# A gated two-branch decoder layer on one core: each weight block loaded once from ScalarE's queue, and gates that meet the branch outputs on chip

## The chip, the cores and the metric

The kernel runs on one core of one Trainium2 chip. The metric is the device time in microseconds (us) of one execution, here simply the time of that core. Engines are called as in the profile: PE (TensorE matmul) with PEld (its weight load), DVE (VectorE), ACT (ScalarE), POOL (GpSimd) and SP (SyncE, which here does nothing but issue DMAs). A row of the profile that begins with SPq is SP handing a DMA to its queue.

## The reference, cut to what matters

```python
D_MODEL = 1024; SEQ = 2048; HG_HEADS = RET_HEADS = 8; HG_DK = 128; RET_DK = 64
h    = rms_norm(x, norm_g) * (1 + scale) + shift          # shift, scale, gate from c @ w_ada
proj = h @ w_in                                           # (2048, 1024) @ (1024, 9216)
(hq, hf, hi, hz, rq, rk, rv, rz, ga, gb) = split(proj)
oA = hgrn2_chunkwise(hq, hf, hi, lower_bounds)            # gated linear recurrence, 8 heads
uA = head_rms_norm(oA, hg_norm_g) * silu(hz)
oB = retention_chunkwise(rotary(rq), rotary(rk), rv)      # decayed linear attention, 8 heads
uB = head_rms_norm(oB, ret_norm_g) * silu(rz)
m  = sigmoid(ga) * uA + sigmoid(gb) * uB
out = rms_norm(x + gate * (m @ w_out), final_g)
```

All of it is in float32.

## The kernel before

**Quads and products.** The projection is done over two superblocks of 1024 positions (`sb`), each of two blocks of 512 (`tb`). Its 9216 columns are cut into 36 "quads" of 256 columns, and a quad of one superblock is a 2x2 arrangement of blocks: two column halves (`ch`) by two position blocks (`tb`). It is computed with seven products instead of eight (a Strassen scheme), numbered m = 1 to 7. The weight of a quad has four blocks, 0 to 3 (128 columns by half of the 1024 rows each); the seven products need block 0 (m=1), block 2 (m=2 and, later, part of a sum), block 3 (m=3), a sum of blocks 0 and 1 (m=5), that sum plus block 3 (m=6), that plus block 2 (m=4), and block 1 plus block 3 (m=7). Each operand is split into a high and a low part (`split_into`: a copy on ACT, then a subtraction on DVE), and a product is 4 x 3 matmuls of 128x128 by 128x512: the group "x12" of the timelines. The split weights wait in the tiles `b`, of which there are three (NBW), so that splits run about three products ahead of PE.

**Kinds of quads.** There are five: "a" (query and forget gate of an HGRN2 head), "v" (values of both branches of a head), "b" (queries and keys of a pair of retention heads, to be rotated), "A" and "B" (the gates of a head's HGRN2 and retention output). `quads_of` sets them in the order a, v, (b for even heads), A, B, head after head. `product_order` interleaves the products of neighbouring quads: ... (1,q) (3,q) (6,q) (2,q+1) (7,q) (5,q+1) (4,q) ... `after` turns a finished product into one of the four results of its quad and passes it on to `take_a`, `take_v`, `take_b` or `take_g`. The last result, of m=4, is read straight from the PSUM bank in which PE summed it (`x`), and the bank is free for the next quad's product when that reading is done.

**Weights.** `Weights.load` issues all loads from SP (256 KB each, tiles `w`, `wz`, `wt`, `wt5n`, `wt6n`). The sums of blocks are made by loading a block a second or third time into a temporary and adding it on DVE (`add`, line 401). In all nine loads per quad.

**Background.** Between the products, a scheduler in the program (`bg`, one burst every GAP ticks, four ticks per product) emits the recurrences: `tree` (the decay tree of a head, matmuls `lv`), `hgrn_out` (chunks `poh`, which read `vh` from DRAM), `retention` (chunks `rt` and `por`, which read `rqk`, `rkz` and `vr`). Layout changes go through DRAM: values are stored in 128-byte pieces to `vd`, rotated keys to `kzd`, branch outputs to `ud`. `merges` reads a head's stored gate (`gd` to `mg`) and output (`ud` to `mu`), multiplies and adds them and stores `mT`, which the last stage (`out_half`, matmuls `ops`) reads.

**Rotation.** `tables` writes the cosines and sines of all positions to `rot` by 128 small DRAM-to-DRAM copies (line 618). `take_b` loads `ct` and `sn` from it when a result of a b quad arrives, then multiplies the result with them on DVE (lines 629 to 632); the result of m=4 stays in its PSUM bank meanwhile:

```python
        ct, sn, sw = tmp(f"ct{nm}"), tmp(f"sn{nm}"), tmp(f"sw{nm}")
        nc.sync.dma_start(out=ct, in_=rot[0, b])
        nc.sync.dma_start(out=sn, in_=rot[1, b])
```

Every engine and every queue works through its instructions in the order in which they stand; that order is made when the program is built. All DMAs of the kernel before are issued by SP.

## Time and profile before

| | |
|---|---|
| median of two runs | 2619.3 us (2616.39 to 2622.2) |
| profiled execution | 2623.15 us, of which the span from first to last instruction is 2621.3 us |
| PE busy | 2008.0 us (77% of the span) |
| DVE, ACT, POOL busy | 1537.3, 941.4, 203.4 us |
| mean granted TensorE clock | 0.883 of full speed |
| DMA | 426.20 MB, mean 163 GB/s; 16 DMA engines busy 59% of the span |

The page has the busy time of the engines, then the span in 40 slices, the DMA queues, the chain of work that ended last, and groups of instructions. A group's row gives the line, engine, operation, output and input names and shapes, the count, busy time and mean duration in ns, and after the second bar the idle time of the engine before these instructions with what ended it. A wait row says which engine and line waited for which: total us, times, longest.

### The profile page before, as it was taken

Reading aid. Unit: us, or ns where it says so; the run is one execution under the profiler, and the core shown is the slowest. Engines: PE = TensorE matmul, PEld = TensorE weight load, DVE = VectorE, ACT = ScalarE, POOL = GpSimd, SP = SyncE. Lnnn points to the kernel's source line nnn. Section 1 sums busy time; section 2 is a strip of 40 time slices with the busy share of each in tenths; the row PEclk is TensorE's granted clock in tenths of the full one; section 3 lists DMA queues with packets and bytes.
Section 4 is the critical chain, followed back from the end, with each engine's and each line's share of the span. In section 5 each row is a group of like instructions: output and inputs, shape, how many; then the busy total and the mean of one; then the engine's idle time right before and its main releaser. Section 6 shows DMA issues by size and latency. Waiting matters only on the chain. (4 is left out here: it accounts for less than half of the span.)

```text
span 2621.3 us, 40791 instructions
## 1 busy us (share of the span) xinstructions
PE 2008.0 (77%) x14648; PEld 1596.4 (61%) x14648; DVE 1537.3 (59%) x2935; ACT 941.4 (36%) x2340; POOL 203.4 (8%) x386
## 2 busy tenths in 40 slices
PE   4337998589866887487675998589867888497998
PEld 2226776477745766375564776367655666375877
DVE  5327576557555666566665666557564766467443
ACT  5312343244423453243532443134423343145332
POOL 1000001000100111000010001000100011000200
PEclk9668999799888998798787999789988999798999
DMA  7125566555656576577865556555666566556763
GB/s 251 41 66 149 148 176 147 143 169 155 158 151 172 147 221 171 155 243 223 237 154 136 156 152 159 147 153 156 162 154 169 152 196 168 146 155 176 190 174 127
DMA packets 904986, 426.20 MB, mean 163 GB/s; under 512 B 419920, under 2 KB 829520, under 8 KB 904784
## 3 DMA queue, kind: packets, MB, share of 16 engines
q1 hardware_dynamic: 904784, 423.60, 59.3%
q8 instruction: 116, 1.90, 0.3%
q14 instruction: 86, 0.70, 0.1%
HBM read 321.73 MB, written 103.81 MB: 162 GB/s over the span
## 5 line engine op out<-in xcount | busy, mean ns | idle before, releaser
L82 PE MATMUL x<-S,b 128*128 128x512 f32 x1704 | 453.4, 412 | 173.0 <-ACT b L303 161.4
L82 PEld LDWEIGHTS x<-S,b 128*128 128x128 f32 x1704 | 331.4, 199 | 254.0 <-ACT b L303 169.2
L82 PE MATMUL x<-A,b 128*128 128x512 f32 x1704 | 440.4, 409 | 23.7 <-DVE c L498 6.3
L82 PE MATMUL v<-S,b 128*128 128x512 f32 x1728 | 449.4, 405 | 8.5 <-DVE b L304 6.4
L82 PEld LDWEIGHTS x<-A,b 128*128 128x128 f32 x1704 | 328.9, 197 | 98.0 <-ACT A L303 7.2
L82 PEld LDWEIGHTS v<-S,b 128*128 128x128 f32 x1728 | 330.2, 195 | 80.8 <-DVE b L304 7.7
L82 PE MATMUL y<-A,b 128*128 128x512 f32 x852 | 247.4, 440 | 157.5 <-DVE ct L631 109.7
L82 PEld LDWEIGHTS y<-A,b 128*128 128x128 f32 x852 | 178.5, 215 | 204.4 <-issue 142.9
L304 DVE TENSOR_TENSOR b<-w,b 128x512 fp32r<-128x512 f32 (+1 forms) x320 | 199.8, 634 | 130.8 <-ACT b L303 128.1
L303 ACT ACTIVATE b<-wz 128x512 fp32r<-128x512 f32 (+1 forms) x240 | 137.8, 584 | 295.4 <-DVE wz L401 203.6
L303 ACT ACTIVATE b<-w 128x512 fp32r<-128x512 f32 (+1 forms) x320 | 183.0, 583 | 163.3 <-PE x L82 80.8
L304 DVE TENSOR_TENSOR b<-wz,b 128x512 fp32r<-128x512 f32 (+1 forms) x240 | 150.4, 635 | 120.6 <-ACT b L303 118.8
L82 PE MATMUL ops<-wo,m 128*128 128x512 f32 x768 | 179.7, 394 | 7.7 <-ACT m L303 4.8
L82 PEld LDWEIGHTS ops<-wo,m 128*128 128x128 f32 x768 | 144.7, 190 | 39.5 <-ACT m L303 5.2
L181 POOL TENSOR_SCALAR ssh<-ssh 128x1 f32<-128x1 f32 x128 | 38.4, 300 | 1501.3 <-ACT jkh L802 1501.2
L474 ACT ACTIVATE c<-v 128x512 f32<-128x512 f32 x144 | 85.7, 595 | 157.4 <-PE v L82 157.0
L802 ACT ACTIVATE jkh<-poh 128x128 f32<-128x128 f32 x128 | 35.2, 275 | 265.9 <-DVE st L871 209.2
L401 DVE TENSOR_TENSOR wz<-wz,wt5n 128x512 f32<-128x512 f32 x72 | 49.5, 687 | 120.2 <-DMA wt5n<-in_w_a_dram 81.2
L733 DVE TENSOR_TENSOR q<-q,f 128x512 f32<-128x512 f32 x112 | 77.0, 688 | 48.2 <-PE lv L82 47.0
L184 POOL TENSOR_TENSOR rrr<-ssr,mhalf 128x2 f32<-128x2 f32 x64 | 51.1, 799 | 620.6 <-DVE ssr L183 503.6
L82 PE MATMUL poh<-vh,k 128*128 128x128 f32 x240 | 53.9, 308 | 51.4 <-DMA vh<-vd 40.7
L82 PEld LDWEIGHTS lv<-q,k 128*32 128x32 f32 (+1 forms) x5888 | 73.0, 113 | 30.3 <-issue 24.3
(186 smaller groups left out, 2599.2 us busy)
## 6 DMA issues: line engine op xcount, KB each, us to landing
w<-in_w_d_dram SPq DMA_DIRECT2D x128, 256.0 KB
w<-in_w_a_dram SPq DMA_DIRECT2D x64, 256.0 KB
w<-in_w_c_dram SPq DMA_DIRECT2D x64, 256.0 KB
vd<-vt SPq DMA_DIRECT2D x256, 64.0 KB
wt<-in_w_d_dram SPq DMA_DIRECT2D x64, 256.0 KB
gd<-c SPq DMA_DIRECT2D x64, 256.0 KB
ud<-ut SPq DMA_DIRECT2D x64, 256.0 KB
mg<-gd SPq DMA_DIRECT2D x64, 256.0 KB
```

The lines of the kernel that those rows point to most:

```text
L82: return tc.keep_in_program_order(nc.tensor.matmul(**kw))
L181: G.tensor_scalar(out=ss, in0=ss, scalar1=1.0 / n, scalar2=EPS, op0=ALU.mult, op1=ALU.add)
L184: G.tensor_tensor(out=dst, in0=ss, in1=mhalf.broadcast_to([P, width]), op=ALU.pow)
L303: S.activation(out=t[0], in_=src, func=AF.Copy)
L304: return V.tensor_tensor(out=t[1], in0=src, in1=t[0], op=ALU.subtract)
L401: V.tensor_tensor(out=t, in0=t, in1=w, op=ALU.add)
L474: S.activation(out=t, in_=ps, func=AF.Copy)
L733: V.tensor_tensor(out=qv, in0=qv, in1=tv[:, :, :, 0:1].broadcast_to([P, NU, nb, m]), op=ALU.mult)
L802: S.activation(out=junk, in_=pos[i], func=AF.Square, accum_out=ss[:, i : i + 1])
```

## The change

- **Weights.** Each block is loaded once per quad (of a superblock) into one of five tiles `r`; only blocks 0 and 2 of the first three quads are loaded a second time. The loads are issued from ScalarE's queue (line 404 of the changed kernel). The sums are made from the resident tiles: before the split of m=5 the sum of blocks 0 and 1, before the split of m=6 block 3 is added to it, after that split block 2 gets the sum added (for m=4) and block 1 gets block 3 added (for m=7). That is four DVE additions per quad, as before.
- **Order of quads.** A written-out order (`ORDER`) puts a head's gate quads A and B about two heads later. A gate's product chain now ends on chip: `fetch_u` loads the stored branch output (`mu`) shortly before, and `take_g` multiplies gate, gain and output and adds the two branches; `merges`, `gd` and the reloads `mg` are gone.
- **Rotation.** `tables` writes 12 copies to a compact table `lin`; `load_rot` loads `ct` and `sn` once per block of positions of a b quad, with a broadcast read, before the products m=1 and m=6 of that quad. The rotation of the m=4 result uses tables that were loaded before.
- **Fewer transfers.** `vr` of two heads is one DMA instead of two, and it and `rkz` are fetched one burst before they are used.
- **Constants.** Factors 1/n and the like are folded into other constants; the eps addition of the retention norm moves from DVE to POOL. The junk output of the squares goes to PSUM. GAP goes from 8 to 7, temporaries (NTP) from 7 to 5, with four tiles `mu`.

```diff
-NR = 3
-NZ = 2
+NR = 5
-NTP = 7
+NTP = 5
-GAP = 8.0
+GAP = 7.0
+ORDER = """a0 v0 b0 v1 a1 b1 v2 a2 A0 B0 v3 a3 A1 B1 v4 b2 a4 A2 B2 v5 a5 A3 B3 v6 b3 a6 A4 B4 v7 a7 A5 B5 B6 A6 B7 A7"""
...
-        def add(self, t, q, b, nm):
-                w = tmp(f"wt{nm}")
-                nc.sync.dma_start(out=as_src(w), in_=wsrc(q, b))
-                V.tensor_tensor(out=t, in0=t, in1=w, op=ALU.add)
...
+        def load(self, reserve=1):
+            while self.nload < len(self.order) and self.free > reserve:
+                q, b = self.order[self.nload]
+                t = self.raw[q, b] = self.tile(f"w{q}_{b}")
+                nc.scalar.dma_start(out=as_src(t), in_=wsrc(q, {11: 0, 12: 2}.get(b, b)))
                 self.nload += 1
...
+                if m == 5:
+                    b11, b12 = have(q, 0), have(q, 1)
+                    z = self.raw[q, 5] = self.tile(f"wz{q}")
+                    self.add(z, b11, b12)
+                elif m == 6:
+                    self.add(have(q, 5), have(q, 5), have(q, 3))
...
+                if m == 6:
+                    self.add(have(q, 2), have(q, 2), have(q, 5))
+                    self.add(have(q, 1), have(q, 1), have(q, 3))
...
-                        nc.sync.dma_start(
-                            out=rot[i, b][32 * g : 32 * g + 32, :].rearrange("d (c j a) -> j d c a", j=4, a=32)[j],
...
+                for j in range(4):
+                    nc.sync.dma_start(
+                        out=lin[i + two].rearrange("d (c j a) -> j d c a", j=4, a=32)[j],
...
+    def load_rot(q, tb):
+        nc.sync.dma_start(out=ct, in_=lin[0, :, sl].unsqueeze(0).broadcast_to([4, 32, BLK]))
+        for two in range(2):
+            nc.sync.dma_start(
+                out=sn[64 * two : 64 * two + 64, :], in_=lin[1 + two, :, sl].unsqueeze(0).broadcast_to([2, 32, BLK])
+            )
...
     def take_b(sb, p, s, tb, z):
-        ct, sn, sw = tmp(f"ct{nm}"), tmp(f"sn{nm}"), tmp(f"sw{nm}")
-        nc.sync.dma_start(out=ct, in_=rot[0, b])
-        nc.sync.dma_start(out=sn, in_=rot[1, b])
+        ct, sn = rots[tb]
...
-        nc.sync.dma_start(out=gd[s, h, b], in_=g)
-        gsent[s, h, b] = bg.now
+        u = mus.pop((s, tb))
+        V.scalar_tensor_tensor(
+            out=u, in0=g, scalar=gnt[:, s * H + h : s * H + h + 1], in1=u, op0=ALU.mult, op1=ALU.mult
+        )
...
+        if kind in "AB" and m in (2, 1):
+            fetch_u(q, 2 - m)
+        if kind == "b" and m in (1, 6) and q >= FIRST:
+            load_rot(q, m // 6)
```

**What moves on SP at the start.** Before, in SP's order right after the cosines and sines have come in (`tabd` holds the turned tables, `wt5n` and `wt6n` are weight blocks for sums):

```order
L618 DMA rot_2_313<-tabd_0_817 128x1x32 x16
L618 DMA rot_2_317<-tabd_0_823 128x1x32 x8
L618 DMA rot_2_317<-tabd_1_826 128x1x32 x8
L618 DMA rot_3_314<-tabd_0_817 128x1x32 x16
L618 DMA rot_3_318<-tabd_0_823 128x1x32 x8
L618 DMA rot_3_318<-tabd_1_826 128x1x32 x8
L400 DMA wt5n_975<-in_w_a_dram 128x4x128
L400 DMA wt6n_984<-in_w_a_dram 128x4x128
L400 DMA wt5n_1004<-in_w_c_dram 128x4x128
```

The same place on SP in the changed kernel, from the tables to the first stores of values:

```order
L614 DMA tab_725<-in_cos_dram 128x512
L614 DMA tab_733<-in_sin_dram 128x512
L621 DMA lin<-tabt_726 512x1x32 x4
L621 DMA lin<-tabt_734 512x1x32 x4
L621 DMA lin<-tab_733 512x1x32 x4
L632 DMA ct_0_746<-lin 128x1x512
L634 DMA sn_0_747<-lin 64x1x512 x2
L599 DMA vd_0_122<-vt_0_0_0_858 32x16x32 x4
```

The 128 small copies are 12, and no weight stands behind them.

**What moves on SP at a b quad.** Before, at the third b quad of the first superblock (`rd` and `kzd` are stores of rotated results, `dk` and `k` the tree's turned keys; `w_22`, `wz`, `wt5n` and `wt_22` weights):

```order
L639 DMA rd_0_286<-ct_2_0_6456 2x32x512 x2
L1005 DMA mu_3_1_6527<-ud_3_1_167 32x16x32 x3
L1003 DMA mg_3_1_6533<-gd_3_1_263 128x512
L1005 DMA mu_3_1_6534<-ud_3_1_199 32x16x32 x4
L627 DMA ct_2_0_6562<-rot_0_311 128x512
L628 DMA sn_2_0_6563<-rot_0_315 128x512
L419 DMA wz_6680<-in_w_d_dram 128x4x128
L411 DMA w_22_6730<-in_w_d_dram 128x4x128
L784 DMA dk_0_0_6786<-f_0_5772 128x512
L400 DMA wt5n_6576<-in_w_d_dram 128x4x128
```

The third b quad in the changed kernel, on SP:

```order
L632 DMA ct_0_4976<-lin 128x1x512
L634 DMA sn_0_4977<-lin 64x1x512 x2
L599 DMA vd_0_130<-vt_4_0_1_4974 32x16x32 x4
L874 DMA vh_0_4_5028<-vd_0_128 128x128
L655 DMA rd_0_214<-c_15_4885 2x32x512 x2
L632 DMA ct_1_5050<-lin 128x1x512
L634 DMA sn_1_5051<-lin 64x1x512 x2
L860 DMA ud_3_0_158<-ut_3_0_5041 128x512
```

The tables of the first block of positions now stand ahead of the quad's first store and those of the second right behind it, and no weight stands in this queue. In all, SP has 2,557 DMAs before and 1,582 after.

**What moves on ACT.** ScalarE's order before, with the numbers in the names, at the quad behind that b quad (`b1_22` is the high part of the split weight for m=1 of quad 22, `c2` and `c5` are copies of finished products out of PSUM, `sz` the sigmoid of a gate):

```order
L303 ACTIVATE b5_22_6845<-wz_22_6680 128x512
L659 ACTIVATE sz0_4_0_6795<-c2_21_6640 128x512
L474 ACTIVATE c2_22_6867<-y22_6844 128x512
L303 ACTIVATE b4_21_6869<-wz_21_6324 128x512
L303 ACTIVATE b1_22_6899<-w1_22_6730 128x512
L668 ACTIVATE c5_21_6725<-c5_21_6725 128x512
L802 ACTIVATE jkh4_0_6891,ssh4_0_6889<-poh4_0_6885 128x128
L805 ACTIVATE uh4_0_6884<-poh4_0_6885,rrh4_0_6890 128x128
L474 ACTIVATE c5_22_6924<-v22_6898 128x512
```

The same in the changed kernel, at its third b quad, number 15 (`w15_3` is weight block 3 of quad 15; `poh` and `uh` belong to the norm of an HGRN2 chunk):

```order
L301 ACTIVATE b5_15_4851<-wz15_4852 128x4x64 x2
L850 ACTIVATE poh3_0_4865,ssh3_0_4869<-poh3_0_4865 128x128
L853 ACTIVATE uh3_0_4864<-poh3_0_4865,rrh3_0_4870 128x128
L486 ACTIVATE c2_15_4885<-y15_4850 128x512
L301 ACTIVATE b4_14_4887<-w14_2_4455 128x512
L404 DMA w15_3_4911<-in_w_b_dram 128x4x128
L301 ACTIVATE b1_15_4906<-w15_0_4779 128x4x64 x2
L404 DMA w16_2_4990<-in_w_a_dram 128x4x128
L486 ACTIVATE c5_15_4942<-v15_4905 128x512
L301 ACTIVATE b3_15_4944<-w15_3_4911 128x4x64 x2
L850 ACTIVATE poh3_1_4918,ssh3_1_4923<-poh3_1_4918 128x128
```

In the kernel before ACT has no DMA; now 294 stand among its copies, and block 3 is issued one product (one `c` copy) ahead of the split that reads it.

More of the change, by code (lines that the diff above doesn't have):

```diff
@@ L403, in load @@
[L403 to L421 removed]
+            self.free = NR
@@ L423, in split, with have, drop, add @@
+        def have(self, q, b):
+            while (q, b) not in self.raw:
+                if not self.free:
+                    raise RuntimeError(f"no weight tile for {QUADS[q]} {b}")
+                self.load(0)
+            return self.raw[q, b]
+        def drop(self, q, b):
+            del self.raw[q, b]
+            self.free += 1
+        def add(self, out, x, y):
+            V.tensor_tensor(out=out, in0=x, in1=y, op=ALU.add)
         def split(self, t):
             m, q = seq[self.nsplit]
-            src = self.raw.pop((m, q)) if m in (1, 2, 3, 7) else self.z[q]
+            have = self.have
@@ L650, in take_b, with fetch_u @@
         bg.post(4.0, store)
-    gpart = {}
+    gpart, mus, half = {}, {}, {}
+    def fetch_u(q, tb):
+        sb, kind, h = QUADS[q]
+        s, b = "AB".index(kind), sb * NBLK + tb
+        n = 0
+        while usent.get((s, h, b), bg.now) > bg.now - 5.0:
+            bg.force()
+            n += 1
+            if n > 400:
+                raise RuntimeError(f"no u {s} {h} {b}")
+        if n:
+            print("forced u", s, h, b, n)
+        ut = mus[s, tb] = upool.tile([P, 512], F32, name=f"mu{s}_{h}_{b}", tag="mu", bufs=4)
+        for i in range(4):
+            nc.sync.dma_start(
+                out=ut[32 * i : 32 * i + 32, :].rearrange("e (c j t) -> e c j t", c=4, j=4),
+                in_=ud[s, h, b].rearrange("(j e) (c i t) -> i e c j t", j=4, c=4, i=4)[i],
+            )
     def take_g(sb, h, s, ch, tb, z):
@@ L1155, in opening @@
         late_consts()
-        for _ in tables():
-            pass
+        tables()
+        load_rot(2, 0)
         for q in range(FIRST):
```

225 lines of the change are left out of this document (92 added, 133 removed).

## The prediction

> **What bounds the kernel now.** I begin with the page's busy times and with the busy time in stretches of the span that I chose by the program's stages: opening, a gap, the products, the output stage, the tail; the last two rows are 29 us inside the products, at a b quad.
>
> ```profile
> PE 2008.0 (77%) x14648; PEld 1596.4 (61%) x14648; DVE 1537.3 (59%) x2935; ACT 941.4 (36%) x2340; POOL 203.4 (8%) x386
> 0.00:95.00 95.00, 49.21 (x164) 33.48 (x164) 63.52 (x126) 55.99 (x89) 10.07 (x26) 0.91 0.57 189
> 95.00:177.00 82.00, 0.24 (x2) 0.12 (x1) 0.83 (x2) 1.39 (x3) 0.00 (x0) 0.52 0.20 37
> 177.00:2421.00 2244.00, 1769.15 (x13614) 1408.49 (x13614) 1385.96 (x2640) 820.66 (x2085) 172.94 (x324) 0.89 0.62 166
> 2421.00:2614.00 193.00, 188.91 (x869) 154.29 (x870) 84.72 (x164) 62.65 (x164) 19.79 (x35) 0.99 0.58 167
> 2614.00:2621.30 7.30, 0.48 (x3) 0.06 (x1) 2.30 (x5) 0.72 (x1) 0.55 (x1) 0.73 0.19 72
> 755.00:770.00 15.00, 11.36 (x51) 7.85 (x49) 7.65 (x15) 2.14 (x5) 0.00 (x0) 0.80 0.22 54
> 770.00:784.00 14.00, 0.00 (x0) 0.00 (x0) 6.26 (x9) 0.38 (x2) 0.00 (x0) 0.50 0.74 206
> ```
>
> A row of stretches has the bounds and length, the busy us of PE, PEld, DVE, ACT and POOL with counts, the granted clock (1 is full), the DMA engines' busy share and GB/s. PE is the engine to watch, and it isn't full. Busy time by clock tells how much matmul work a stretch holds at full clock: 1769.15 x 0.89 = 1575 us in the 2244 us of products, 70%; in the output stage 188.91 x 0.99 = 187 us in 193 us, 97%. So some 670 us of the products' stage are lost to waits and to slow clock, and PE stands for 82 us before it. Who ends PE's waits:
>
> ```profile
> PE x L82 <- ACT b L303: 167.5, 10, 81.8
> PE y L82 <- DVE ct L631: 109.7, 6, 20.3
> PE poh L82 <- DMA vh<-vd: 63.4, 11, 13.2
> PE rt L82 <- DMA rqk<-rd: 48.0, 11, 11.5
> PE y L82 <- DVE vt L582: 20.4, 5, 7.0
> PE y L82 <- DVE f L562: 18.9, 1, 18.9
> PE poh L82 <- DMA k<-dk: 10.7, 4, 3.9
> ```
>
> These 439 us are most of PE's idle time outside the opening's first 95 us. The timeline shows what stands behind the first two; first the gap at 95 us:
>
> ```profile
> 95.57 76.42 SPq L618 DMA_DIRECT2D rot<-tabd  x119
> 172.04 0.65 SPq L400 DMA_DIRECT2D wt5n<-in_w_a_dram  x1
> 176.89 4.57 PE L82 MATMUL x<-S,b 128*128 128x512 f32 x12 [81.75 <-ACT b L303]
> 181.29 2.88 PE L82 MATMUL v<-S,b 128*128 128x512 f32 x12
> 184.01 2.88 PE L82 MATMUL x<-S,b 128*128 128x512 f32 x12
> ```
>
> A weight block stands behind 119 copies that SP hands over at 0.64 us each (76.42 / 119), while the DMA engines are 20% busy. SP's issuing is the bound there. The last two rows give the price of a warm product, 184.01 - 181.29 = 2.72 us, and the row above that of the first one after a stop: about 4.4 us until the next starts. Then a b quad:
>
> ```profile
> 765.39 1.12 SPq L639 DMA_DIRECT2D rd<-ct  x2
> 778.50 0.61 SPq L400 DMA_DIRECT2D wt5n<-in_w_d_dram  x1
> 782.92 0.69 DVE L401 TENSOR_TENSOR wz<-wz,wt5n 128x512 f32<-128x512 f32 x1 [0.90 <-DMA wt5n<-in_w_d_dram]
> 784.39 4.60 PE L82 MATMUL x<-S,b 128*128 128x512 f32 x12 [14.94 <-ACT b L303]
> 795.93 6.14 SPq L644 DMA_DIRECT2D kzd<-sw  x4
> 802.11 1.01 SPq L627 DMA_DIRECT2D ct<-rot  x1
> 806.06 0.68 DVE L629 TENSOR_TENSOR sw<-x,sn 64x512 f32<-64x512 f32 x1 [6.40 <-DMA sn<-rot]
> 808.32 4.57 PE L82 MATMUL y<-A,b 128*128 128x512 f32 x12 [19.34 <-DVE ct L631]
> ```
>
> Two stops in one chain of SP. A store of a rotated result waits for DVE at the head of the queue, then scattered loads go out, so the weight `wt5n` is issued at 778.5 and PE starts 14.94 us late. Then `ct` and `sn` for the m=4 result are issued behind four scattered stores that take SP 6.14 us; the result holds its PSUM bank until DVE has them, and PE stands 19.34 us more. Seven of the eight b quads show the second stop (the rows of 109.7 and 18.9 us are these seven).
>
> **The change, part by part.**
>
> *Opening.* With 12 copies and no weight behind them on SP, the 81.75 us go, and 4.57 becomes 2.72. Twelve issues at 0.64 us are 7.7 us, beside products. Left may be a weight that lands late; between 0 and one landing (rows below, 8.7 us) I keep 6. Term: **-78 us**.
>
> *b quads.* Stops by late weights: 167.5 - 81.75 = 86 us. By late tables: 109.7 + 18.9 = 129 us. After each of some 14 stops the first product costs 1.9 us more (4.60 against 2.72): 27 us. Together 242. What is late next: the tables of a block are now issued one product (2.72 us) before the first result that needs them; three issues (1.9 us) and a landing of 3.4 us (a weight's, rows below) can make DVE wait 1.9 + 3.4 - 2.72 = 2.6 us, eight times: +20. Term: **-222 us**.
>
> *Late `vh`, `rqk` and `k`.* 63.4 + 48.0 + 10.7 = 122 us. They too wait their turn on SP, which had 2,557 DMAs and has 1,582; the weights, the gates' round trip and half of the tables are gone from it. But they are loads of what was stored a few us earlier, and the scattered stores stay. Between none and all I take three quarters, since the longest (13.2 and 11.5 us) are of the size of the stops above: 92 us, with 1.9 us of slow clock for 13 of the 26 waits, an estimate, 25 us. Term: **-117 us**.
>
> *DVE.* Additions for sums are four per quad in both kernels:
>
> ```profile
> L401 DVE TENSOR_TENSOR wz<-wz,wt5n 128x512 f32<-128x512 f32 x72 | 49.5, 687 | 120.2 <-DMA wt5n<-in_w_a_dram 81.2 <-DMA wt5n<-in_w_c_dram 19.1 <-DMA wt5n<-in_w_d_dram 17.0
> L1015 DVE SCALAR_TENSOR_TENSOR mg<-mg,gnt,mu 128x512 f32<-128x512 f32 x64 | 47.7, 745 | 60.8 <-DMA mu<-ud 60.7
> ```
>
> The two gate instructions per head and block stay too, so DVE's work is unchanged; the small ones that move to POOL (8% busy) are nothing. DVE's waits for these DMAs outside the opening (120.2 - 81.2 and 60.7) get shorter, and with them the 20.4 us in which PE waited for a transpose out of its bank: **-15 us**. The multiplication by `mu` now stands in the chain of a gate, but after the reading of its bank, and `mu` is issued six products (16 us) ahead.
>
> *ACT.* What it pays for the loads comes from SP's rows for them, and their landing from the chain of waits:
>
> ```profile
> L411 SPq DMA_DIRECT2D w<-in_w_d_dram x128: 601/613/2078, 182.9 to 2365.3; - x128
> SPq L411 <- DVE b L304: 96.0, 56, 8.2
> 1955.10 3.36 DMA wz<-in_w_d_dram
> 1984.33 4.81 DMA wt6n<-in_w_d_dram
> 2276.65 8.73 DMA wt5n<-in_w_d_dram
> ```
>
> 294 x 0.613 = 180 us on an engine that is 36% busy: 941 + 180 is about half of the new span. The danger is the wait before it: SP waited 1.7 us each (96.0 / 56) until DVE had read the tile that a load overwrites. On ACT this stops the splits and the copies that free PSUM banks. With five tiles, the last block of a quad is issued only when block 0 has been split. From there, 0.6 (issue) + 4.8 (landing) + 0.6 (copy) + 0.7 (subtraction) = 6.7 us pass, and PE needs the block three products, 8.2 us, later. So it is covered by 1.5 us; without that cover every us costs 72 us. From 0 to 294 x 2.3 us (wait and issue, all on the path) I take the low end, near the cover: **+20 us**.
>
> *DMA volume.* 354 weight loads, 128 gate transfers and 32 table loads less, at 256 KB, are 135 MB of 426. That changes nothing where SP's order was the bound (20% and 22% busy in the rows above), and helps where scattered pieces fill the engines (74%).
>
> *Temporaries and pace.* Five temporaries for seven stand against four per merge and four per b quad that are no longer taken; GAP 7 for 8 spreads the same background over fewer ticks. I put both at nothing; the tile waits that they can add are in the rivals.
>
> [...] The trace has a product after a stop at 4.4 to 4.6 us against 2.72, and a clock of 0.50 in the stretch where PE stood. [...]
>
> [...]
>
> **Sum.** Against the profiled execution's 2623 us: -78 -222 -117 -15 +20 = 2211. The median of the two runs is 4 us lower: 2207. A second way: the products' stage without the terms above is 2244 - 334 = 1910 us for 1575 us of work, 82%, which leaves PE still far from the 97% of the output stage. Since fewer stops also shorten those small waits that I left alone, I go a little lower: **2190 us**.
>
> **The rivals.**
>
> 1. *Background keeps pace.* If SP's relief ends nearly all waits for DMA, the products run at 90%: 1575 / 0.9 = 1750, with 95 + 193 + 7 and a few us, **2050**. For it: the output stage runs at 97% with background beside it. Against: waits on DVE's own chains stay, and the scattered stores.
> 2. *The DMA engines were the bound.* Then weights at b quads come as late from the other queue, and only the gap at 95 us and the direct wait for tables go: 2619 - 78 - 129 = **2412**. For it: 74% busy in the row at 770 us. Against: 22% in the 15 us before, when the delay arose.
> 3. *The last block comes late.* If landings beside scattered traffic take longer than the cover, as the 8.73 us row, a quad loses 8.73 - 4.81 - 1.5 = 2.4 us, 72 quads 175 us: **2365**.
> 4. *ACT becomes the blocked queue (slower).* Its place: the load between two splits that waits for DVE, which waits for a split of ACT. At 1.7 + 0.6 us for each of 294, wholly on PE's path, 2190 + 676 = **2866**. It decides from the point where a load costs PE 1.65 us: 2190 + 294 x 1.65 = 2675, 2% above the run before. Against: splits run three products ahead.
>
> **How the numbers follow.** A measurement of this kernel tells about 2% from no change. Chances: forecast 0.56 (its own range 2090 to 2290), first rival 0.14, second 0.11, third 0.13, fourth 0.06. The range 2050 to 2380 takes in the forecast, the first rival's time and the third's, and leaves out the second, the fourth and the tail below the first. All but the fourth, and a little of a mixture with it, are faster by over 2%: faster 0.91, same 0.04, slower 0.05.
>
> **What would show it.** Right: no stop of PE between 95 and 180 us; no row in which PE waits for DVE's rotation, and few waits of `y` at b quads; waits for `vh` and `rqk` below 50 us together; ACT's idle time before splits ended by PE, not by DMA; stretches of products with a clock of 0.95. Wrong: "PE x <- ACT b" spread over all quads with ACT waiting for a weight's landing (third rival) or DVE's waits for ACT grown (fourth); 14 us stops at b quads with the weights' landing times doubled (second); or a new long wait of DVE for `mu` or for a temporary, which no row of before could show.

## The result and the profile after

The changed kernel takes **2391.1 us** (2390.39 to 2391.85, two runs) against 2619.3: ratio 0.913, 95% interval 0.908 to 0.917. The forecast was 2190 us, 2050 to 2380. The direction was right, the gain was 228 us of the 429 forecast, and the time lies just above the range.

The busy times of the page, and four stretches of the span, cut by the same stages as before the change (opening, products, the gap ahead of the output stage, that stage):

```profile
PE 1981.6 (83%) x14648; PEld 1576.2 (66%) x14648; DVE 1518.7 (64%) x2858; ACT 943.5 (40%) x2340; POOL 219.9 (9%) x466
0.00:97.00 97.00, 44.21 (x153) 29.59 (x154) 60.96 (x120) 53.80 (x86) 8.16 (x24) 0.93 0.49 164
97.00:2186.00 2089.00, 1760.60 (x13728) 1401.14 (x13728) 1367.97 (x2590) 828.27 (x2129) 199.08 (x410) 0.93 0.46 117
2186.00:2204.40 18.40, 0.00 (x0) 0.00 (x0) 18.31 (x32) 10.69 (x18) 0.00 (x0) 0.58 0.66 208
2204.40:2382.00 177.60, 176.80 (x768) 145.41 (x768) 69.82 (x116) 50.04 (x109) 11.83 (x30) 0.99 0.45 140
```

The same 14648 matmuls are in both kernels, so the first row splits the gain of the span (2621.3 - 2388.6 = 232.7 us): PE's busy time fell by 26.4 us (the mean granted clock went from 0.883 to 0.929), its idle time from 613 to 407 us, by 206. What ended PE's waits (total us, times, longest):

```profile
PE poh L77 <- DMA vh<-vd: 67.6, 15, 13.0
PE poh L77 <- DMA k<-dk: 60.2, 16, 18.3
PE rt L77 <- DVE rs L1011: 59.8, 38, 10.1
PE ops L77 <- ACT m L301: 18.6, 1, 18.6
PE lv L77 <- DVE ad L794: 17.5, 9, 8.4
PE y L77 <- DVE ro L647: 6.6, 2, 3.7
PE x L77 <- ACT b L301: 2.0, 2, 1.2
```

The last two rows are what is left of the two largest kinds of stop before: 128.6 us for rotated results and 167.5 us for late weights are gone, and `rqk` (48.0) has no row left. But `vh` is where it was (63.4), `k` has gone from 10.7 to 60.2, `rs` from 30.6 to 59.8, and the wait at the entry of the output stage is 18.6 us for 4.8. One of the longest of these waits, in the timeline of SP's queue, in two stretches of it, and in the chain that ended last:

```profile
545.86 1.09 SPq L655 DMA_DIRECT2D rd<-c  x2
547.78 3.27 SPq L634 DMA_DIRECT2D sn<-lin  x2
551.09 0.98 SPq L860 DMA_DIRECT2D ud<-ut  x1
552.12 5.57 SPq L874 DMA_DIRECT2D vh<-vd  x3
565.08 0.68 DVE L645 TENSOR_TENSOR sw<-c,sn 64x512 f32<-64x512 f32 x1 [13.25 <-DMA ud<-ut]
555.00:560.00 5.00, 0.00 (x0) 0.00 (x0) 0.00 (x0) 0.00 (x0) 0.00 (x0) 0.72 0.28 91
560.00:565.00 5.00, 0.00 (x0) 0.00 (x0) 0.00 (x0) 0.00 (x0) 0.00 (x0) 0.50 0.28 68
552.12 13.07 DMA vh<-vd
```

For 10 us no engine works, and yet the DMA engines are busy 28%: a share of 0.28 is 4.5 of 16, and from 561 to 563 us it is 0.13, 2.1 of 16. It is not SP that is full here, and not the 16 engines together. A few engines still had work, and a 256 KB store (`ud`) and loads of `vh`, issued at 551 and 552, landed only at 565. Two kinds of transfers in this kernel have a short dimension in front: the new table loads (`ct` read over 4 groups, `sn` over 2) and the stores of a rotated result, `rd` (2 halves), which the kernel before has too. Each of them is seen with next to nothing else under way: `ct` (issued at 113.04 us) and two `sn` (issued at 533.37 and 533.97) in the changed kernel, and in the kernel before the `rd` stores that SP issued at 765.39 us. The last row is the stretch of the stop above:

```profile
116.00:117.50 1.50, 1.13 (x3) 0.94 (x4) 1.45 (x3) 0.32 (x1) 0.00 (x0) 0.50 0.26 93
539.00:540.50 1.50, 0.30 (x2) 0.00 (x0) 0.09 (x1) 0.00 (x0) 0.00 (x0) 1.00 0.13 49
770.50:771.00 0.50, 0.00 (x0) 0.00 (x0) 0.00 (x0) 0.00 (x0) 0.00 (x0) 0.50 0.13 49
561.00:563.00 2.00, 0.00 (x0) 0.00 (x0) 0.00 (x0) 0.00 (x0) 0.00 (x0) 0.50 0.13 48
```

Shares of 0.26, 0.13 and 0.13 are 4.2, 2.1 and 2.1 of 16 engines. The runs below agree: splitting these transfers into pieces with 32 in front saves 30 and 53 us.

**Theory**: the missing 200 us are waits behind few-engine transfers. **Rivals**: SP's queue itself (loads behind stores that wait for DVE), pacing (a load planned too few ticks ahead of its use), DVE full at b quads. And, for the gain itself: the queue, the tables' lead, the order, or the transfers that went.

### The profile page after: what moved, and what is told of

Its sections match the earlier page's. It is cut to its first block, busy times and chain, and to the rows that moved or that the text cites. A ratio compares the mean times of both kernels' runs of the same rounds, so it can differ in the third digit from the quotient of the medians.

```text
span 2388.6 us, 39722 instructions
## 1 busy us (share of the span) xinstructions
PE 1981.6 (83%) x14648; PEld 1576.2 (66%) x14648; DVE 1518.7 (64%) x2858; ACT 943.5 (40%) x2340; POOL 219.9 (9%) x466
## 4 chain that ended last, share of the span: by engine, by line
PE 38%; DMA 23%; DVE 20%; ACT 7%; issue 5%; SPq 3%; POOL 3%; ACTq 1%; DVEq 0%; POOLq 0%
PE x L77 13%; PE ops L77 7%; PE v L77 6%; DMA w<-in_w_d_dram 6%; DVE b L302 5%; PE y L77 5%; DMA w<-in_w_c_dram 3%; ACT b L301 3%; PE poh L77 2%; DMA k<-dk 2%; DMA w<-in_w_a_dram 2%; PE rt L77 2%; DMA w<-in_w_b_dram 2%; DMA vh<-vd 2%; DVE wz L419 2%
## 5 line engine op out<-in xcount | busy, mean ns | idle before, releaser
L77 PE MATMUL x<-S,b 128*128 128x512 f32 x1704 | 443.4, 405 | 7.7 <-DVE c L499 3.2
L302 DVE TENSOR_TENSOR b<-w,b 128x512 fp32r<-128x512 f32 (+1 forms) x400 | 250.2, 634 | 212.5 <-ACT b L301 211.1
L77 PEld LDWEIGHTS x<-S,b 128*128 128x128 f32 x1704 | 325.3, 195 | 81.6 <-ACT b L301 5.3
L301 ACT ACTIVATE b<-w 128x512 fp32r<-128x512 f32 (+1 forms) x400 | 229.6, 584 | 191.5 <-PE x L77 89.8
L77 PE MATMUL y<-A,b 128*128 128x512 f32 x852 | 239.4, 427 | 10.2 <-DVE ro L647 6.6
L77 PE MATMUL ops<-wo,m 128*128 128x512 f32 x768 | 176.8, 393 | 18.6 <-ACT m L301 18.6
L302 DVE TENSOR_TENSOR b<-wz,b 128x512 fp32r<-128x512 f32 (+1 forms) x160 | 100.2, 634 | 98.8 <-ACT b L301 97.9
L301 ACT ACTIVATE b<-wz 128x512 fp32r<-128x512 f32 (+1 forms) x160 | 92.0, 585 | 166.8 <-PE x L77 50.8
L850 ACT ACTIVATE poh<-poh 128x128 f32<-128x128 f32 x128 | 33.5, 262 | 280.1 <-DVE st L919 241.5
L77 PEld LDWEIGHTS poh<-vh,k 128*128 128x128 f32 x240 | 43.4, 205 | 152.7 <-DMA vh<-vd 59.7
L419 DVE TENSOR_TENSOR wz<-wz,w 128x512 f32<-128x512 f32 x72 | 49.8, 691 | 115.7 <-DMA w<-in_w_d_dram 55.9
L77 PE MATMUL lv<-q,k 128*32 128x16 f32 (+2 forms) x5888 | 81.6, 188 | 33.0 <-DVE ad L794 17.5
```

The lines of the kernel that those rows point to most:

```text
L77: return tc.keep_in_program_order(nc.tensor.matmul(**kw))
L301: S.activation(out=t[0], in_=src, func=AF.Copy)
L302: return V.tensor_tensor(out=t[1], in0=src, in1=t[0], op=ALU.subtract)
L419: V.tensor_tensor(out=out, in0=x, in1=y, op=ALU.add)
L850: S.activation(out=junk, in_=pos[i], func=AF.Square, accum_out=ss[:, i : i + 1])
```

## The experiments

| kernel | us | ratio to before, 95% |
|---|---|---|
| split table loads | 2360.9 | 0.901 [0.899, 0.904] |
| split table loads and `rd` stores ("split kernel") | 2307.9 | 0.882 [0.880, 0.883] |
| changed, weights from SP | 2389.0 | 0.913 [0.911, 0.915] |
| split kernel, weights from SP | 2299.5 | 0.878 [0.875, 0.880] |
| split kernel, loads planned earlier | 2322.6 | 0.887 [0.883, 0.890] |
| split kernel, `vh` and `k` from GpSimd's queue | 2275.8 | 0.870 [0.867, 0.873] |
| the same, `k` used later | **2260.7** | 0.863 [0.860, 0.866] |
| the same, part of the rotation on GpSimd | 2291.1 | 0.875 [0.873, 0.878] |
| split kernel, rotation cut | 2261.0 | 0.863 [0.859, 0.867] |
| split kernel, GAP 8 | 2330.0 | 0.890 [0.887, 0.893] |
| split kernel, idle copies added | 2404.7 | 0.919 [0.915, 0.922] |
| before, `rd` stores split | 2541.0 | 0.970 [0.967, 0.974] |
| before, weights from ScalarE | 2616.2 | 1.000 [0.999, 1.002] |
| before, tables a product earlier | 2614.1 | 0.998 [0.997, 1.000] |
| before, stores split and early tables | 2534.5 | 0.967 [0.965, 0.969] |
| before, these two and weights from ScalarE | 2524.3 | 0.964 [0.962, 0.966] |
| before, new order of quads | 2675.6 | 1.022 [1.018, 1.025] |
| before, all four | 2609.0 | 0.997 [0.995, 0.999] |

**Few engines.**

```diff
-        nc.sync.dma_start(out=ct, in_=lin[0, :, sl].unsqueeze(0).broadcast_to([4, 32, BLK]))
+        for g in range(4):
+            nc.sync.dma_start(out=ct[32 * g : 32 * g + 32, :], in_=lin[0, :, sl])
```

(`sn` likewise.) 

> The changed kernel, with the loads of the rotation tables split into pieces of 32 rows (four for ct, four for sn, each from contiguous rows of 512 columns), in place of reads broadcast over 4 and 2 groups. Theory 'few engines': the broadcast reads run on only 4 and 2 of the 16 DMA engines, everything queued behind them on those engines (k, vh, the store's pieces) lands some us later, and that is part of the 128 us in which PE waits for vh and k. Then the rows for k and vh fall by 20 to 60 us and the time to 2330 to 2375. Theory 'pacing' (a load is simply planned too few ticks ahead of the matmul that needs it): k and vh stay within 10 us of 60 and 68, time 2380 to 2400. Theory 'SP's issues are the bound': five more DMAs per block, 80 in all at 0.6 us, make it up to 20 us slower.

The second kernel splits the stores too:

```diff
-            for two in range(2):
-                nc.sync.dma_start(out=dst[two], in_=r[64 * two : 64 * two + 64, :])
+            for g in range(4):
+                nc.sync.dma_start(out=dst[g // 2][g % 2], in_=r[32 * g : 32 * g + 32, :])
```

> As the run with split tables, and the stores of the rotated result too go out in four pieces of 32 rows instead of two of 64 with a split dimension in front. Theory 'few engines': no DMA of a b quad is left on 2 or 4 engines; the 14 us from issue to landing of a ud store beside a b quad falls to about 5, k and vh together fall below 70 us, time 2300 to 2350, at least 15 us below the tables alone. Theory 'pacing': within 10 us of the changed kernel. Theory 'SP's issues': 144 more DMAs in all, 10 to 40 us slower.

The third is the kernel before with the second of these edits: 

> The kernel before, with one edit: the stores of the rotated result go out in four pieces of 32 rows in place of two of 64 with a split dimension in front. Theory 'few engines' (two pieces of 128 KB on 2 of 16 engines, eight per b quad, hold back the weights and tables behind them): PE's two stops at b quads (86 us for weights, 129 us for tables) shrink by a third or more and the time falls from 2616 to 2500 to 2560. Theory 'SP's order is the bound, as the prediction had it': the stops stay within 20 us, 2595 to 2620.

The bytes are the same and the DMAs are more, and the times fell by 30 and 53 us, and by 73 in the kernel before, all three times inside what "few engines" expected. What it does to SP is seen at the scattered stores of `kzd`, which stand right behind the `rd` stores. Rows of that tile (duration in ns: min/median/max) come first from the kernel before, then, with a stretch of SP's timeline and PE's wait for a rotated result, from the same with split stores, then from the changed kernel and from the split kernel:

```profile
L644 SPq DMA_DIRECT2D kzd<-sw x64: 322/962/4175, 236.1 to 2264.1; - x64
```

```profile
L644 SPq DMA_DIRECT2D kzd<-sw x64: 303/504/561, 237.8 to 2181.5; - x64
760.01 2.03 SPq L644 DMA_DIRECT2D kzd<-sw  x4
PE y L82 <- DVE ct L631: 65.6, 6, 12.9
```

```profile
L660 SPq DMA_DIRECT2D kzd<-sw x64: 303/1036/3769, 158.2 to 1928.4; - x64
```

```profile
L659 SPq DMA_DIRECT2D kzd<-sw x64: 302/502/1100, 165.6 to 1844.9; - x64
```

Four `kzd` stores took SP 6.14 us in the row that the prediction showed; they take 2.03 here. So they were slow because of the store in front of them, not because they are scattered. PE's waits for a rotated result fell with it from 109.7 to 65.6 us; late weights fell less, from 86 to 74 (155.2 - 81.6). In the split kernel no transfer to or from `ud` takes over 5.4 us to land, where one took 14 us above. One expectation missed: `k` and `vh` together are at 101 us for 128, not below 70:

```profile
PE 1965.8 (85%) x14648; PEld 1565.2 (68%) x14648; DVE 1521.0 (66%) x2858; ACT 942.7 (41%) x2340; POOL 222.3 (10%) x466
PE poh L77 <- DMA k<-dk: 55.1, 16, 11.9
PE poh L77 <- DMA vh<-vd: 45.8, 13, 6.9
```

The rest of the 83 us is in many small rows and in 15.8 us less busy time. With the tables alone split, `vh` and `k` were at 92.7 us already, so splitting the stores as well did not lower them. Few-engine transfers thus explain 83 of the 200 us, and only a third of that through `vh` and `k`.

**What holds back `vh` and `k`.** Four runs on the split kernel. More program time between load and use (of `k`, then of `vh`, with one more fetched ahead):

```diff
-            while bb not in age or bg.now < age[bb] + 9.0:
+            while bb not in age or bg.now < age[bb] + 20.0:
-            while nf < CH and nf <= n + 1:
+            while nf < CH and nf <= n + 2:
-                    if n in age and bg.now >= age[n] + 6.0:
+                    if n in age and bg.now >= age[n] + 12.0:
```

> The kernel with split tables and split stores (2307.9 us; PE waits 55 us for k and 46 us for vh), with more program time between a load and the matmul that needs it: k is used 20 ticks after its load is issued for 9 (a tick is a quarter of a product, 0.68 us), vh 12 ticks for 6, and vh is fetched two pieces ahead for one. Theory 'pacing': k and vh together fall from 101 to below 40 us and the time to 2230 to 2260. Theory 'SP is held up by the stores in front of the loads, by an amount that a few us do not cover': k and vh stay above 70 us, 2290 to 2320. Rival on the other side: the background falls behind by the added ticks and is made up in bursts, 2320 to 2380.

Another queue for the two loads (`nc.sync` to `nc.gpsimd` at both):

> The kernel with split tables and split stores, with the loads of vh and k alone issued from GpSimd's queue (256 loads), so that they stand behind no store that waits for DVE. Theory 'SP is held up by the stores in front of the loads': k and vh fall from 101 to below 50 us, time 2240 to 2275. Theory 'pacing or the DMA engines': k and vh stay at 80 to 120 us, time 2290 to 2330. Rival: GpSimd, which makes the factors that PE waits for (rb, 24 us) and the root of each norm, is held up by loads of its own: its waits grow and the time is 2330 or more.

Less work for DVE:

```diff
-        V.tensor_tensor(out=sw[64:128, :], in0=z[0:64, :], in1=sn[0:64, :], op=ALU.mult)
-        V.tensor_tensor(out=sw[0:64, :], in0=z[64:128, :], in1=sn[64:128, :], op=ALU.mult)
         V.tensor_tensor(out=r, in0=z, in1=ct, op=ALU.mult)
-        V.tensor_tensor(out=r, in0=r, in1=sw, op=ALU.add)
```

> The kernel with split tables and split stores; three of the four instructions of the rotation are left out (the two products with sn and the sum), so the rotated result is not computed; transposes, stores and loads stay. It takes 32 blocks x 3 x 0.69 = 66 us of DVE out of the b quads. Theory 'DVE is full at a b quad, and the stores that wait for it hold up SP and with it k and vh': k and vh fall from 101 to below 60 us, waits for rs too, time 2230 to 2265. Theory 'scattered stores alone hold up SP' or 'pacing': the waits stay within 20 us, time 2285 to 2310.

PE's waits with more program time, then with GpSimd's queue, then with the rotation cut:

```profile
PE poh L77 <- DMA vh<-vd: 44.0, 5, 15.5
PE rt L77 <- DMA rqk<-rd: 16.4, 4, 11.0
PE rt L77 <- DMA vr<-vdr: 15.0, 4, 5.4
```

```profile
PE poh L77 <- DMA k<-dk: 47.1, 14, 8.3
```

```profile
PE poh L77 <- DMA vh<-vd: 53.2, 22, 6.5
PE poh L77 <- DMA k<-dk: 52.6, 15, 11.7
```

More program time removed the row of `k`, and other loads came late instead: 15 us slower, inside the range of the rival by which the background falls behind, so pacing alone falls. (Three edits at once: which of them cost is not shown.) On GpSimd's queue `vh` has no row left and 32 us are gone, to within 0.8 us of the theory's range: SP's queue held it. `k` stays at 47; its data are first stored, by SP, behind the same stores, which may be why, but no run tests it. Cutting 64 us of DVE's work (1521.0 to 1456.6 busy) brought 47 us, but left `vh` and `k` at 106: DVE is one of the things late at b quads, by another way than the theory said. For what is left of `k`, pacing was tried again, now that SP stood no longer in front:

```diff
-            while bb not in age or bg.now < age[bb] + 9.0:
+            while bb not in age or bg.now < age[bb] + 15.0:
```

> The kernel with split tables and stores and with vh and k loaded from GpSimd's queue (2275.8 us; k 47 us, vh below 8), and k used 15 ticks after its load for 9 (4 us more), since its waits are 3.4 to 4.6 us but for one. Theory 'what is left of k is pacing, once no store of SP is in front': k falls below 15 us, 2235 to 2255. Theory 'a wait that goes comes back elsewhere' (as in the run with more program time on SP's queue): k falls, but vh, rqk, vr or rs rise by as much, 2265 to 2290.

```profile
PE poh L77 <- ACT uh L852: 28.3, 3, 17.1
PE poh L77 <- DMA k<-dk: 7.9, 2, 6.6
```

`k` is down to 7.9 us and 15 us are gained, 6 us short of the expected time, so what was left of it was pacing. But 28 us of waits for ACT (the scaling of an HGRN2 chunk) have come up. At 2260.7 us this is the fastest kernel found. Moving part of the rotation off DVE failed:

```diff
+        E = V if (s, tb) == (0, 1) else G
-        V.tensor_tensor(out=sw[64:128, :], in0=z[0:64, :], in1=sn[0:64, :], op=ALU.mult)
+        E.tensor_tensor(out=sw[64:128, :], in0=z[0:64, :], in1=sn[0:64, :], op=ALU.mult)
```

(the second product likewise.) 

> The fastest kernel so far (2260.7) with the two half-width products of the rotation on GpSimd for the results that lie in SBUF (24 blocks, 48 instructions, 33 us of DVE). Leaving out 66 us of DVE there gave 47. Theory 'DVE is full at b quads': 2235 to 2255. Rival 'GpSimd, which now also waits for landings of its own loads, returns them late': 2262 to 2300.

The instruction's row on GpSimd, with its durations, and the wait that came back:

```profile
L645 POOL TENSOR_TENSOR sw<-c,sn x24: 1255/1290/1832, 127.5 to 1821.5; 64x512 f32<-64x512 f32 x24
PE poh L77 <- DMA k<-dk: 24.4, 3, 14.0
```

1.29 us in place of 0.68, on the engine that now also issues `k`: 30 us slower.

**The queue.** The changed kernel with one word changed in `Weights.load` (`nc.scalar` to `nc.sync`): 

> The changed kernel with its weight loads issued from SP again, all else as it is (each weight once, summed on chip). Theory 'the second queue is what removed the late weights': PE's wait for a split at b quads comes back, 3 to 10 us at each of 8 quads plus smaller ones, time 2430 to 2500. Theory 'the order and the fewer transfers did it, the queue is nothing': within 1% of 2391. If ACT's issuing (about 300 x 0.6 us) sits on the path, it is faster: 2330 to 2380.

The reverse, in the kernel before, at all three sites of its loads: 

> The kernel before with nothing changed but the queue: every weight block and every block for a sum is issued from ScalarE's queue. By the prediction's terms: the stop of 81.75 us at the opening goes, or shrinks to what the tables' copies leave, the late weights at b quads (86 us and some 14 us of slow first products) go, the late tables (129 us) stay: 2619 - 78 - 86 - 14 = 2440, range 2400 to 2480. Rival 'the loads block ACT' (648 loads that wait for DVE to have read the tile): slower than 2619. Rival 'DMA engines': only the opening's stop goes, 2540.

Once more, in the split kernel: 

> The kernel with split tables and stores (2307.9 us), its weight loads issued from SP again instead of ScalarE. Before the split, the queue made no difference (2389.0 against 2391.1). Theory 'the queue is worth nothing here': 2295 to 2320. Theory 'the second queue pays once no DMA is left on 2 or 4 engines, since SP's order is then the bound': weights come late again, 2335 to 2400. Theory 'ACT's issuing costs more than SP's order': 2250 to 2290.

Three times the queue made no difference of over 0.5% (nor does it in a fourth pair below, 2534.5 and 2524.3 us). The prediction's terms, 2400 to 2480 for the kernel before, are refuted by that, and none of that run's rivals came either. Its two sides are seen in the changed kernel with weights from SP:

```profile
PE v L77 <- ACT b L301: 103.0, 20, 15.1
PE poh L77 <- DMA k<-dk: 31.8, 15, 4.4
PE poh L77 <- DMA vh<-vd: 26.9, 5, 14.9
```

Weights are late by 103 us, and `k` and `vh` wait 59 us in place of 128: in the time in which PE stands for a weight, the other loads land. And in the kernel before with weights from ScalarE, the late weights at b quads stay (95.5 us for 86), so SP's order was not what made them late. The opening's stop of 81.75 us is a shorter one with another name, since values still wait behind the tables' copies on SP; the 30 us gained there come back in waits elsewhere:

```profile
PE x L82 <- ACT b L303: 95.5, 10, 21.1
189.54 1.62 PE L82 MATMUL y<-A,b 128*128 128x512 f32 x3 [52.19 <-DVE vt L582]
```

**Parts of the change alone.** Early tables in the kernel before:

```diff
+        if QUADS[q][1] == "b":
+            if m == (5 if q < FIRST else 1):
+                load_rot(q, 0, 0)
+            elif m in (4, 6, 7):
+                load_rot(q, int(m > 4), int(m != 6))
```

> The kernel before with one part of the change alone: at a b quad the two table blocks of a result are loaded one product (2.72 us) before the result is ready, from SP as before, as whole blocks. The prediction's term: PE's stops of 109.7 + 18.9 us go, and half of the 27 us of slow first products: 2616 - 129 - 13 = 2475, range 2460 to 2500. Rival 'the stop is the scattered stores in front of whatever SP has to issue': the stop shrinks by 2.7 us at each of eight, some 20 to 40 us, 2570 to 2600. Rival 'a stop that goes uncovers the next': the waits for tables go, those for weights, vh and k grow, 2540 to 2600.

SP's timeline there, and PE's stop:

```profile
788.03 6.72 SPq L656 DMA_DIRECT2D kzd<-sw  x4
794.79 2.00 SPq L633 DMA_DIRECT2D ct<-rot  x1
802.03 4.42 PE L82 MATMUL y<-A,b 128*128 128x512 f32 x12 [19.64 <-DVE ct L643]
```

A load that stands one product earlier in the program is still issued when SP gets there; neither the forecast of that run nor its rivals came. Two and three edits together: 

> The same without the edit of the queue: split stores and early tables, weights from SP. Theory 'one hold-up behind another': late tables go (66 us of stops in the run with split stores alone), the weights stay late behind SP, 2465 to 2500. Theory 'parts add up': 2520 to 2560.

> The kernel before with three edits that were run alone: the rotated result's stores in four pieces (alone 2541.0), the tables loaded one product earlier (alone 2614.1) and the weights from ScalarE's queue (alone 2616.2). Theory 'one hold-up behind another': each edit is worth what the prediction gave it once the others are gone: the opening's stop shrinks by 30 or more, late weights and late tables at b quads (155 - 82 and 66 us in the run with split stores) nearly go, 2616 - 75 - 30 - 73 - 66 + something that comes back = 2370 to 2430. Theory 'parts add up': 2616 - 75 - 2 - 0 = 2539, 2520 to 2560.

The parts add up; they do not hide one another (0.970 of the time before with split stores, 0.967 with early tables too, 0.964 with the queue too). The order of the quads, as one line in place of `quads_of`, alone and with the three:

```diff
-QUADS = [(sb, kind, n) for sb in range(NSB) for kind, n in quads_of(sb)]
+QUADS = [(sb, x[0], int(x[1])) for sb in range(NSB) for x in ORDER.split()]
```

> The kernel before with one part of the change alone: the order of the quads (v and a quads two heads ahead, gates A and B two heads late). Weights, tables, gates' round trip through memory and all queues stay as before. Theory 'the order is what ended the stops at b quads' (between a b quad and the next use of its neighbours' data stand other quads, so that SP gets through its row): the stops for weights (86 us) and tables (129 us) fall by half or more, 2616 - 110 = 2450 to 2540. Theory 'it is the transfers that went (weights once, no gates through memory)': 2590 to 2640.

> The kernel before with four edits together: the new order of the quads, the rotated result's stores in four pieces, early tables, weights from ScalarE's queue (2524.3 without the order). What is left to the changed kernel with split stores and tables (2307.9) is then: each weight once, gates without the round trip, 12 copies for 128, tiles. Theory 'order': 2360 to 2450, most of the way. Theory 'transfers': 2500 to 2540, so that the 135 MB less are worth some 200 us.

With the order alone, what ended PE's waits:

```profile
PE poh L74 <- DMA k<-dk: 128.3, 13, 14.5
PE x L74 <- ACT b L295: 116.2, 12, 81.9
PE poh L74 <- DMA vh<-vd: 88.6, 10, 26.3
PE y L74 <- DVE ct L623: 25.9, 3, 15.6
```

The late weights at b quads did fall (116.2 - 81.9 = 34 us, 86 before), and so did the waits for rotated results (25.9 us for 128.6): the order alone ends most of the stops at b quads. But `k` rose by 118 us and `vh` by 25, and the time by 61, beyond both ranges expected; with the three other edits the order costs 85 us (2609.0 for 2524.3), again beyond both. So in the kernel before the order costs, the queue and the tables' lead bring nothing, and some 300 us (2609.0 to 2307.9) come from what is left: weights loaded once, gates without their round trip, 12 copies for 128, the tables loaded once per block, the fewer and earlier loads of `vr` and `rkz`, the tiles, and GAP 7 for 8. Three things can be read of it. GAP is worth 22 us in the split kernel (under "Pace"). With four edits a stop of 49.1 us at the opening still stands, and PE waits 150.1 us for `k`, where the split kernel has 55.1:

```profile
185.08 1.62 PE L74 MATMUL y<-A,b 128*128 128x512 f32 x3 [49.10 <-DVE vt L579]
PE poh L74 <- DMA k<-dk: 150.1, 13, 17.0
```

Which edit shortened the wait for `k` is not shown. To tell bytes from places, transfers whose data nobody uses were added to the split kernel:

```diff
                 nc.scalar.dma_start(out=as_src(t), in_=wsrc(q, {11: 0, 12: 2}.get(b, b)))
+                nc.scalar.dma_start(out=as_src(dram(f"cp{q}_{b}", [P, 512])), in_=wsrc(q, {11: 0, 12: 2}.get(b, b)))
```

> The kernel with split tables and stores (2307.9 us) and, behind each weight load, a second transfer of the same 256 KB from memory to a scratch place in memory, from ScalarE's queue, which nobody waits for: some 300 transfers and 77 MB more, nothing else. The transfers that the change took away were 514 and 137 MB. Theory 'the bytes cost' (about 300 us between the kernel with four edits and this one, by the share of the bytes 300 x 77 / 137): 2440 to 2500. Theory 'what cost was not the bytes but who stands in SP's row and who waits for a landing': 2300 to 2345.

This run did not answer that. The copies were all placed in the first 498 us. The same stretch with and without them:

```profile
97.00:480.00 383.00, 268.23 (x2212) 213.65 (x2213) 214.82 (x415) 121.52 (x304) 26.65 (x50) 0.84 0.93 250
```

```profile
97.00:480.00 383.00, 329.24 (x2826) 261.28 (x2826) 256.74 (x503) 149.54 (x403) 39.20 (x79) 0.93 0.46 109
```

With the copies PE gets through 2212 matmuls for 2826 in the stretch (78%), and the run takes 97 us more. Two causes are mixed in that. The DMA engines were full (0.93 busy); and ACT, which issues the copies, did no other work while it handed out as many as 14 in a row:

```profile
233.83 14.31 ACTq L405 DMA_DIRECT2D cp<-in_w_d_dram  x14
247.23 0.76 PE L77 MATMUL poh<-vh,k 128*128 128x128 f32 x2 [29.34 <-DMA cp<-in_w_d_dram]
248.79 0.26 ACT L850 ACTIVATE poh<-poh 128x128 f32<-128x128 f32 x1 [30.34 <-DVE st L917]
```

This stop of PE and two more of the kind (23.4 and 16.1 us, behind 8 and 12 copies in a row) come to 69 us together, in a run that is 97 us longer. For 294 transfers the 97 us are 0.33 us each, by which 514 would be some 170 us of the 300. That is an estimate from a denser stretch than any of the kernel before, with ACT's part in it, so it does not say what the bytes cost.

**Pace.** GAP 8 for 7: 

> The kernel with split tables and stores (2307.9 us) with the background every 8 ticks, as before the change, for every 7. The prediction put this at nothing: 2295 to 2320. Theory 'the denser background is what comes too early for its loads': k, vh and rs fall from 152 to below 110 us, 2265 to 2290. Rival: the lanes fall behind the order of the quads and are made up in bursts, 2330 or more.

Slower by 22 us, the rival's time. `k` (62.9) and `vh` (41.2) together stay where they were, 104 us for 101, so the denser background is not what makes them late; that the lanes fell behind is the rival's reason, and no row shows it.

## Why the prediction was right or wrong

*Opening, -78.* Right in size. The first product behind the gap starts at 100.78 us for 176.89; stops of 7.26 us at 116 and 8.42 us at 161 remain, neither ended by a weight's split. It is the copies that left SP, not the weights' queue: the queue alone left a stop of 52 us, and the changed kernel with its weights back on SP has no stop over 8 us between 95 and 180 us.

*b quads, -222.* The stops went as forecast (2.0 and 6.6 us are left of 86 and 129), but for other reasons than it gave. "Four scattered stores that take SP 6.14 us" were held by stores on two engines. The queue and the earlier tables, on which the term rested, bring nothing alone. The order of the quads, which the term does not name, takes both stops down by itself (86 to 34 and 129 to 26 us).

*Late `vh`, `rqk` and `k`, -117.* **This is the step that failed.** 30 us of waits were to be left of 122, because fewer DMAs stand on SP; 128 were left, so the term brought nothing. `rqk` went, `vh` stayed and `k` grew, 128 us for 74 for the two. The new order by itself brings them late (`k` 128.3 and `vh` 88.6 in the kernel before with only the order changed). The stops at b quads had been time in which these loads landed: where weights come late again by 103 us, the two wait 59. And the new table loads put two more kinds of few-engine transfer in front of them (with these split, `vh` 52.0 and `k` 40.7). Only another queue and a later use of `k` took both below 8 us. The text said "the scattered stores stay" and took three quarters all the same.

*Ramps.* 27 and 25 us had been set for the clock. The busy time of the same matmuls fell by 26.4 us: the size of the first term, whose stops went. The second hung on waits for `vh`, `rqk` and `k`, which stayed. In the fastest kernel, where they are nearly gone, busy time is 1952.1 us, 55.9 below before, near the 52 of both terms. That all of it is the clock is not sure: the split kernel has 1965.8 us busy at a mean clock of 0.945, and 1987.6 at 0.942 with its weights from SP. The clock of 0.89 over the stage does not tell the clock of busy time, since it is a mean over idle time too (0.50 in the row in which PE stood). For the same reason 1769.15 x 0.89 = 1575 us is not the matmul work at full clock: the changed kernel's products give 1760.60 x 0.93 = 1637 by that formula, for 13728 matmuls in place of 13614. The second way to the sum and the first rival's 2050 rest on the 1575 and fall with it.

*DVE -15, ACT +20.* Waits for DVE's chains rose instead: `rs` +29 us, `lv` for `ad` 17.5 against 3.0, and the new wait of DVE for a temporary, of which the text warned, came twice (25.8 us for `ud`, row below). ACT's issuing cost next to nothing: from SP the times are 2 and 8 us shorter (2389.0 and 2299.5).

*DMA volume, temporaries, GAP at nothing.* Volume at nothing was wrong by the largest amount, if the 300 us are mostly the transfers', which is not shown; other terms would then have taken the credit. GAP was worth 22 us in the split kernel. Gates two heads late leave the last heads' work with no product beside it: 18.6 us ahead of the output stage, in no term (4.8 before, 13.5 with the order alone).

*The sum.* Against 2190: `vh` and `k` about 98 us (128 - 30), ramps 26, `rs` 29, output stage 14 more than before, and the 17 us that were taken off the sum at the end: 184 of 201. These are the largest pieces and not a full account: DVE's 15 us that did not come, and ACT's 20 and most of the tables' 20 that were not needed, are not among them.

*The rivals.* None came. The second (2412) is nearest in time and its reason was half right, engines held by slow transfers, but its stops at b quads did not stay. A second queue for the weights changed the time by 0.4% at most in the four pairs of runs. For `vh` and `k`, which on SP stand behind stores that wait for DVE, another queue was worth 32 us.

Two rows of the changed kernel, ACT's longest wait before splits and DVE's for a temporary:

```profile
ACT b L301 <- PE x L77: 140.7, 84, 7.2
DVE sw L645 <- DMA ud<-ut: 25.8, 2, 13.3
```

*What would show it.* No stop between 95 and 180 us: right in the main, 7.26 and 8.42 us are left. Rotation: right. `vh` and `rqk` below 50: wrong, and this check named the failure. ACT's idle time before splits ended by PE: right in the main, by the row ahead, with 41 us ended by weights' landings. Clock 0.95: 0.93.

*Open.* Whether the 300 us are bytes or places in SP's queue; what the order would do without the round trip of the gates; and of the 70 us between the fastest kernel and the forecast, how much is DVE: 47 us came from cutting the rotation, on the split kernel, and the two were not tried together.

## What to carry to other kernels

Look at the slowest dimension of every DMA before its bytes: a store split as two halves held the queue behind it, and four plain pieces of the same bytes were worth 53 to 73 us here. A row at the head of a stall names what waits, not what it waits for; where all engines rest and the DMA share is a few sixteenths, look one transfer further back. When a stop is to go, list the loads that land during it, since they are late next, and give each part of a change its own run before it gets its own term.

## What was unexpected in the hardware

`rd` stores of 128 KB with a dimension of 2 in front (2.1 of 16 engines busy in the row at 770.5 us) made SP's next issues slow: median 962 to 1036 ns for a `kzd` store behind it, 502 to 504 without, up to 4.2 us at worst. A pass over 64x512 elements took GpSimd 1.29 us and DVE 0.68. With the DMA engines 93% busy, for 46%, PE got through 78% of the matmuls in the same stretch, but ACT's handing out of the copies has a part in that: 14 of them in a row took it 14.31 us, 1.02 us each, where the issue of a weight load has a median of 0.609 us.
